# First block of a decoder trunk: squares summed by TensorE, condition vector loaded first, two conditioning rows by TensorE

## The chip, the cores and the metric

One Trainium2 chip, one of its cores. The time is device microseconds of one execution of the whole kernel. The engines named below are TensorE (PE, with its weight loads PEld), VectorE (DVE), ScalarE (ACT), GpSimd (POOL) and SyncE (SP), which issues nearly all transfers. Each engine takes its own instructions in order and waits for the others by semaphores.

## The reference

One layer of a conditioned decoder, 2048 tokens of width 1024. A vector c of width 1024 conditions it: six vectors of 1024 come from one product with a 1024 x 6144 matrix.

```python
c_act = jax.nn.silu(c)
mod = (c_act @ w_ada[l] + b_ada[l])[:, None, :]
sh1, sc1, g1, sh2, sc2, g2 = jnp.split(mod, 6, axis=-1)
h = rms_norm(x) * (1.0 + sc1) + sh1
x = x + g1 * token_mixer(h, w_in[l], ...)
h = rms_norm(x) * (1.0 + sc2) + sh2
x = x + g2 * conv_ffn(h, w_up[l], ...)
return rms_norm(x) * final_gain
```

The change is about the first two lines and the first `rms_norm`, for the first 512 tokens.

## The kernel before

The tokens are taken in four blocks of 512 (`TB`), the width in eight tiles of 128 (`KD`), so x of a block is eight tiles `x[k]` of 128 x 512 with the width on the partitions. Every product with weights is made of three TensorE products of fp32r parts: a weight or activation is split into a high part (a ScalarE cast) and a low part (a VectorE subtraction). `h[k]` holds both parts of the normed, scaled and shifted tile.

The 6144 outputs of the conditioning are 48 columns of 128, called rows here, since row m needs the 128 x 1024 tile `wada[m]` with its outputs on the partitions. `ada(m)` makes one on VectorE: one multiply-and-reduce over 128 x 1024 against `c_act`, which holds the conditioned vector on all partitions, and one short read of the accumulator, into column m of `mod`. Rows 0 to 7 are the shift, 8 to 15 the scale of the first norm; tile k needs rows k and 8 + k.

The first block is done by `startup`, written out by hand in the order in which the code stands; the framework's scheduler then sets each engine's own order by priority, which mostly follows it. In the kernel before it runs so. SP issues the vector of constants `vec`, the table `c_all` (it holds the identity `ident`, a causal mask and `ones`), `craw` (c broadcast to 128 partitions), eight transfers of x, and the first rows and weights, in that order; of SP's transfers eight are under way at a time, and the ninth waits for the first. ScalarE makes the sigmoid of `craw`, VectorE multiplies (`c_act`). ScalarE squares each x tile, VectorE adds it to `acc` (`sumsq`), TensorE sums `acc` over the partitions by four products with `ones`, VectorE makes the reciprocal root by three Newton steps, TensorE spreads it by four transposes, and ScalarE copies it to `bc`. Then for each k: `scaled` (VectorE: x times scale times bc), `high` (ScalarE: add the shift, round), `low` (VectorE: the rest), with conditioning rows and weight splits laid between, and `flush`, which gives TensorE the products that have both operands: with `f` and `q` (512 columns each) and with `v` (256 columns for each of four groups of 128 tokens). Row, weight and tile buffers limit how early loads can start: two raw weight buffers (`NRAW`), three for each part, and eight (`NA4`) for rows, `c_act` and `craw`.

The results stand in four accumulator banks of PSUM. The next product, `pshfh` of unit 1, needs one of them, which ScalarE frees by its two activations `sfh` and `snh` of `pshfh`. From there on the kernel runs in a long fixed sequence of products in which rows 16 to 47 are made between other VectorE work.

Of the kernel before, what the change touches and what calls it, by code (L numbers as in the profile page):

```python
# [10 lines left out]
F32 = mybir.dt.float32  # L11
# [7 lines left out]
P = 128  # L19
D = 1024  # L20
SEQ = 2048
KD = D // P
# [82 lines left out]
def trunk(ctx, tc, xT, vecs, cvec, cst, rope, msk, wada, win, walow, wgla, wout, wup, wdown, out):  # L105
# [37 lines left out]

    vec = pc.tile([P, NV], F32, tag="vec", name="vec")
# [6 lines left out]
    nc.sync.dma_start(c_all[:], cst)  # L151
# [25 lines left out]
    craw = pa.tile([P, D], F32, tag="a4k", name="craw")  # L177
    nc.sync.dma_start(craw[:], cvec.to_broadcast([P, D]))
# [210 lines left out]
    def startup():  # L389


        x, W, pending = [], {}, []
        for k in range(KD):
            x.append(x_tile(f"x0_{k}", k))
            nc.sync.dma_start(x[k], xT[0, :, k, :])
        raws = {}
# [20 lines left out]
        def load(*ms):  # L417
            for m in ms:
                raws[m] = ada_load(m, True)
        load(8, 0)  # L420
        weight("f", 1)
        load(9)
        weight("q", 0)
        load(1, 2)
        acc = new_acc("n1_0")
        for k in range(KD):
            sumsq(acc, x[k], k, "n1_0_")
        cond(8)
        ps = late_ps("ssn1_0")
        for c in range(NCH):  # L430
            T.matmul(ps[:, c:c + 1], acc[:, c * P:(c + 1) * P], ones, start=True, stop=True)
# [3 lines left out]
        cast("f")  # L435
# [4 lines left out]
        cond(0)  # L440
        cond(9)
        S.copy(bc[:], ps[:])
        cast("q")
# [19 lines left out]
        def flush():  # L463
            for q in list(pending):
# [4 lines left out]
        plan = [((10,), (), (1,), "f"), ((3, 11), (), (2,), "q"), ((4,), (10,), (3,), "v0"),  # L469
                ((12, 5), (11,), (4,), None), ((13, 6), (12,), (5,), "v1"), ((14, 7), (13,), (6,), None),  # L470
                ((15,), (14,), (7,), None), ((), (15,), (), None)]
        parts = {"f", "q"}, set()
        for k, (ld, first, then, wl) in enumerate(plan):
            if k == 0:
                weight("v0", 2)
            if k == 3:
                weight("v1", 3, True)
            load(*ld)
            for m in first:
                cond(m)  # L480
            scaled(x[k], bc[:], k)
            high(x[k], k, "0_")
            if k in (1, 4):
                name = "v0" if k == 1 else "v1"
                cast(name)
                parts[0].add(name)
            for m in then:
                cond(m)
            low(x[k], k)
            if wl:  # L490
                low_part(wl)
                parts[1].add(wl)
# [1154 lines left out]
```

## Time and profile before

| | |
|---|---|
| median of 3 runs | 2535.63 us (2533.63 to 2539.6) |
| the profiled execution | 2533.2 us |
| its span | 2531.4 us |
| PE busy | 2452.0 us, 97% |
| PEld busy | 2059.3 us, 81% |
| DVE busy | 1989.5 us, 79% |
| ACT busy | 1147.5 us, 45% |
| POOL busy | 146.3 us, 6% |
| HBM read, written | 397.46 MB, 125.30 MB, 207 GB/s over the span |

The page cuts the span into 40 slices of 63 us. TensorE's busy tenths are 5 in the first slice, 9 in all others but two, which have 8. The chain of work that ended last is TensorE for 82% of the span, VectorE for 8%, transfers for 5%. Matmuls are pipelined, and a row of several lasts from the first's start to the last's end. In a timeline row the bracket tells how long the engine was idle before it and what released it; L numbers are lines of the kernel before.

### The profile page before, as it was taken

How to read it: one execution, taken by the hardware profiler on the slowest of the kernel's cores; microseconds unless marked ns; L12 is line 12 of the kernel's file. 1: busy time of each engine (PE TensorE's matmuls, PEld its weight loads, DVE VectorE, ACT ScalarE, POOL GpSimd, SP SyncE). 2: the span in 40 equal slices, each digit the busy share in tenths (PEclk: the TensorE clock that was granted, in tenths of full speed). 3: DMA queues.
4: the chain of work that ended last, by engine and by line, in shares of the span. 5: the costliest groups of instructions: out<-in, count | busy, mean ns of one | idle time of the engine just before them, and what ended most of it. 6: DMA issues, size and time to landing. Idle time of an engine off the chain costs nothing.

```text
span 2531.4 us, 35178 instructions
## 1 busy us (share of the span) xinstructions
PE 2452.0 (97%) x12165; PEld 2059.3 (81%) x12165; DVE 1989.5 (79%) x3652; ACT 1147.5 (45%) x1950; POOL 146.3 (6%) x278
## 2 busy tenths in 40 slices
PE   5999999999999999999999999999989999999998
PEld 4888877888888888788788888888868888888887
DVE  8987887877688685877798888887678777778666
ACT  3334434434443434434554454455445545545442
POOL 1000000000000000000100000000001010010000
PEclk9999999999999999999999999999999999999999
DMA  8844458865689647884654544587665544447663
GB/s 312 296 159 134 169 169 322 290 234 169 215 283 318 224 157 241 311 300 158 222 190 147 171 147 141 168 283 243 209 199 186 159 137 152 150 133 263 213 196 126
DMA packets 232498, 525.11 MB, mean 207 GB/s; under 512 B 24928, under 2 KB 28032, under 8 KB 232320
## 3 DMA queue, kind: packets, MB, share of 16 engines
q1 hardware_dynamic: 229120, 512.38, 60.0%
q0 software_dynamic: 3200, 10.49, 1.2%
q8 instruction: 96, 1.57, 0.2%
q14 instruction: 82, 0.67, 0.1%
HBM read 397.46 MB, written 125.30 MB: 207 GB/s over the span
## 4 chain that ended last, share of the span: by engine, by line
PE 82%; DVE 8%; DMA 5%; issue 2%; ACT 1%; SPq 0%; DVEq 0%; POOL 0%; ACTq 0%; POOLq 0%
PE X L254 6%; PE X L256 6%; PE X L255 6%; PE Z L256 3%; PE Z L255 3%; PE Z L254 3%; PE lvh L662 3%; PE dX L256 3%; PE dX L255 3%; PE dX L254 3%; PE psqkvgr L254 2%; PE psqkvgr L256 2%; PE psqkvgr L255 2%; PE y L254 2%; PE y L256 2%
## 5 line engine op out<-in xcount | busy, mean ns | idle before, releaser
L254 PE MATMUL X<-B,A 128*128 128x512 f32 x572 | 224.4, 392 | 1.4 <-ACT u L1354 1.4
L255 PE MATMUL X<-B,A 128*128 128x512 f32 x572 | 223.9, 391 | 0.0
L256 PE MATMUL X<-B,A 128*128 128x512 f32 x572 | 223.6, 391 | 0.0
L1055 DVE TENSOR_TENSOR dA<-rd,dA 128x512 fp32r<-128x512 f32 x154 | 106.0, 689 | 87.6 <-ACT dA L1054 87.5
L1054 ACT CAST dA<-rd 128x512 fp32r<-128x512 f32 x154 | 95.6, 621 | 138.8 <-PE dY L256 42.2
L1055 DVE TENSOR_TENSOR A<-s,A 128x512 fp32r<-128x512 f32 x176 | 120.7, 686 | 40.7 <-ACT A L1054 40.3
L1054 ACT CAST A<-s 128x512 fp32r<-128x512 f32 x176 | 108.6, 618 | 68.0 <-PE Z L256 45.2
L254 PE MATMUL dX<-dB,dA 128*128 128x512 f32 x352 | 136.9, 389 | 0.0
L255 PE MATMUL dX<-dB,dA 128*128 128x512 f32 x352 | 136.9, 389 | 0.0
L256 PE MATMUL dX<-dB,dA 128*128 128x512 f32 x352 | 136.9, 389 | 0.0
L254 PEld LDWEIGHTS X<-B,A 128*128 128x128 f32 x572 | 108.2, 189 | 24.5 <-ACT u L1354 2.2
L255 PEld LDWEIGHTS X<-B,A 128*128 128x128 f32 x572 | 108.2, 189 | 22.7
L256 PEld LDWEIGHTS X<-B,A 128*128 128x128 f32 x572 | 108.2, 189 | 22.7
L255 PE MATMUL Z<-B,A 128*128 128x512 f32 x308 | 120.0, 390 | 2.2 <-DVE B L1055 2.2
L254 PE MATMUL Z<-B,A 128*128 128x512 f32 x308 | 119.9, 389 | 0.0
L256 PE MATMUL Z<-B,A 128*128 128x512 f32 x308 | 119.8, 389 | 0.0
L662 PEld LDWEIGHTS lvh<-qbh,kh 128*128 128x128 f32 x768 | 100.5, 192 | 17.0 <-issue 9.2
L1055 DVE TENSOR_TENSOR dB<-rb,dB 128x512 fp32r<-128x512 f32 x154 | 105.6, 686 | 10.2 <-ACT dB L1054 10.1
L1055 DVE TENSOR_TENSOR A<-r,A 128x512 fp32r<-128x512 f32 x130 | 89.3, 687 | 29.4 <-ACT A L1054 29.1
L662 PE MATMUL lvh<-qbh,kh 128*128 128x128 f32 x768 | 102.8, 277 | 7.3 <-DVE kh L672 7.1
L1054 ACT CAST A<-r 128x512 fp32r<-128x512 f32 x130 | 81.0, 623 | 62.4 <-PE Z L256 60.0
L254 PE MATMUL psqkvgr<-hqkvgr,ha 128*128 128x512 f32 x256 | 106.1, 415 | 1.1 <-DVE orsg L160 1.0
(475 smaller groups left out, 6981.2 us busy)
## 6 DMA issues: line engine op xcount, KB each, us to landing
gs<-yv SPq DMA_DIRECT2D x154, 256.0 KB, 2.9
rb<-gs SPq DMA_DIRECT2D x154, 256.0 KB, 3.9
r<-wup SPq DMA_DIRECT2D x140, 256.0 KB, 3.3
s<-sumsu SPq DMA_DIRECT2D x136, 256.0 KB, 3.0
wada<-wada SPq DMA_DIRECT2D x48, 512.0 KB, 6.0
rd<-sumsd SPq DMA_DIRECT2D x88, 256.0 KB, 3.8
rd<-wdown SPq DMA_DIRECT2D x66, 256.0 KB, 3.9
x<-xT SPq DMA_DIRECT2D x64, 256.0 KB, 5.8
```

The costliest lines, as they stand in the source:

```text
L254: T.matmul(ps, lhs[0], rhs[0], start=first, stop=False, skip_group_check=more)
L255: T.matmul(ps, lhs[0], rhs[1], start=False, stop=False, skip_group_check=more)
L256: T.matmul(ps, lhs[1], rhs[0], start=False, stop=last, skip_group_check=more)
L662: T.matmul(ps[:, c * P:(c + 1) * P].rearrange("p (h n s) -> p h n s", h=2, s=s), kq[:, c * P:(c + 1) * P], rhs, start=True, stop=True)
L1054: S.copy(hi, src)
L1055: V.tensor_tensor(lo, src, hi, op=ALU.subtract)
```

## The change

The first transfer is now `craw`, and `c_all` goes out on GpSimd's queue. x comes in four transfers of two tiles each, with the first rows between them. `c_act` is transposed by TensorE into eight columns `ccol`. The squares are no longer added by VectorE: for each tile TensorE multiplies the four 128 x 128 pieces of the square with `ones` and accumulates over the tiles in PSUM. Rows 15 and 7 leave VectorE: `row_spread` transposes the row's tile by TensorE in eight pieces, ScalarE copies them, and `row_sum` multiplies them with the columns of `ccol` in eight products of one column; ScalarE adds the bias. The order inside the tiles is a list of strings (`s` scaled, `c` row, `h` high, `l` low, `l` with a name the low part of that weight).

```diff
+    craw = pa.tile([P, D], F32, tag="a4k", name="craw")
+    nc.sync.dma_start(craw[:], cvec.to_broadcast([P, D]))
     vec = pc.tile([P, NV], F32, tag="vec", name="vec")
     nc.sync.dma_start(vec[:], vecs)
...
-    nc.sync.dma_start(c_all[:], cst)
+    nc.gpsimd.dma_start(c_all[:], cst)
...
-        for k in range(KD):
-            x.append(x_tile(f"x0_{k}", k))
-            nc.sync.dma_start(x[k], xT[0, :, k, :])
+        def x_load(i):
+            x.extend((x_tile(f"x0_{2 * i}", 0), x_tile(f"x0_{2 * i + 1}", 1)))
+            nc.sync.dma_start(pair[0][:].rearrange("p (a n) -> p a n", a=2), xT[0, :, 2 * i:2 * i + 2, :])
...
-        load(8, 0)
+        def row_spread(m):
+            raw, halves = raws.pop(m), []
+            for j in range(2):
+                p = lev_ps(f"wt{m}_{j}")
+                for i in range(4):
+                    T.transpose(p[:, i * P:(i + 1) * P], raw[:, (4 * j + i) * P:(4 * j + i + 1) * P], ident)
+                t = tmp(f"wt{m}_{j}")
+                S.copy(t[:], p[:])
+                halves.append(t)
+            return m, halves
+        def row_sum(m, halves):
+            p = late_ps(f"wm{m}")
+            for i in range(KD):
+                T.matmul(p[:, 0:1], halves[i // 4][:, (i % 4) * P:(i % 4 + 1) * P], ccol[:, i:i + 1],
+                         start=i == 0, stop=i == KD - 1)
+            S.activation(mod[:, m:m + 1], p[:, 0:1], AF.Identity, bias=bada1[:, m:m + 1])
+        load(8)
+        x_load(0)
+        x_load(1)
+        load(0)
+        x_load(2)
+        x_load(3)
+        load(9)
         weight("f", 1)
-        load(9)
+        load(1)
         weight("q", 0)
-        load(1, 2)
-        acc = new_acc("n1_0")
+        load(10, 2)
+        cond(8)
+        for j in range(2):
+            p = lev_ps(f"cc{j}")
+            for i in range(4):
+                T.transpose(p[:, i * P:(i + 1) * P], c_act[:, (4 * j + i) * P:(4 * j + i + 1) * P], ident)
+            S.copy(ccol[:, 4 * j:4 * j + 4], p[:, 0:512:P])
+        ps = late_ps("ssn1_0")
         for k in range(KD):
-            sumsq(acc, x[k], k, "n1_0_")
-        cond(8)
-        ps = late_ps("ssn1_0")
-        for c in range(NCH):
-            T.matmul(ps[:, c:c + 1], acc[:, c * P:(c + 1) * P], ones, start=True, stop=True)
+            sq = late(f"sqn1_0_{k}")
+            S.activation(sq[:], x[k], AF.Square)
+            for c in range(NCH):
+                T.matmul(ps[:, c:c + 1], sq[:, c * P:(c + 1) * P], ones, start=k == 0 and c == 0,
+                         stop=k == KD - 1 and c == NCH - 1, skip_group_check=True)
+        cond(0)
...
-        cond(0)
         cond(9)
+        cast("f")
         S.copy(bc[:], ps[:])
-        cast("q")
...
+        loads = [(11,), (3, 15, 12), (7, 4), (13, 5, 14), (6,), (), (), ()]
+        casts = ["q", "v0", None, "v1", None, None, None, None]
+        steps = ["s0 c1 h lf l c10", "s1 h c2 lq l", "s2 h c11 lv0 l", "s3 c3 h c12 l", "s4 c4 h lv1 l c13",
+                 "s5 c5 h c14 l", "s6 c6 h s7 l", "h l"]
...
             pending += [(kind, k, w) for w in (0, 1) for kind in "fqv"]
+            if rows:
+                row_sum(*rows.pop(0))
+            if k in (3, 4):
+                rows.append(row_spread({3: 15, 4: 7}[k]))
             flush()
```

ScalarE, head of the program, before: the exponential for `lbe`, then the sigmoid of c, then the squares (`san` and `sqn`).

```order
L168 ACT_TABLE_LOAD
L168 ACTIVATE lbe<-lbe 128x4
L179 ACT_TABLE_LOAD
L179 ACTIVATE c_act<-craw 128x1024
L355 ACTIVATE san_0_375<-x_0_345 128x512
L358 ACTIVATE sqn_0_1_377<-x_0_345 128x512
```

ScalarE at the same place in the changed kernel; `cc` is the PSUM tile of the transposed `c_act`.

```order
L180 ACT_TABLE_LOAD
L180 ACTIVATE c_act<-craw 128x1024
L170 ACT_TABLE_LOAD
L170 ACTIVATE lbe<-lbe 128x4
L457 COPY ccol<-cc_375 128x4
L457 COPY ccol<-cc_381 128x4
L461 ACTIVATE sqn_0_0_388<-x_0_348 128x512
L461 ACTIVATE sqn_0_1_394<-x_0_348 128x512
```

The two copies into `ccol` now stand between the sigmoid and the squares, and the two table loads have changed places.

VectorE, the first two tiles, before: `x_0_345` holds tiles 0 and 1, the `wada` rows are conditioning rows 1 and 2, `ha` is the low part of a tile, `lf` and `lq` those of the weights.

```order
L365 SCALAR_TENSOR_TENSOR x_0_345<-x_0_345,mod,bc_0_419 128x512
L199 ISA wada_371,mod<-wada_371,c_act,vec 128x1024
L372 SCALAR_TENSOR_TENSOR ha_0_440<-x_0_345,mod,ha_0_440 128x512
L412 TENSOR_TENSOR lf<-rf,hf 128x1024
L365 SCALAR_TENSOR_TENSOR x_0_345<-x_0_345,mod,bc_0_419 128x512
L199 ISA wada_373,mod<-wada_373,c_act,vec 128x1024
...
L372 SCALAR_TENSOR_TENSOR ha_1_455<-x_0_345,mod,ha_1_455 128x512
```

VectorE at the same place in the changed kernel; `wada_364` is row 1, `wada_370` row 10, `wada_372` row 2.

```order
L366 SCALAR_TENSOR_TENSOR x_0_348<-x_0_348,mod,bc_0_451 128x512
L200 ISA wada_364,mod<-wada_364,c_act,vec 128x1024
...
L413 TENSOR_TENSOR lf<-rf,hf 128x1024
L373 SCALAR_TENSOR_TENSOR ha_0_472<-x_0_348,mod,ha_0_472 128x512
L200 ISA wada_370,mod<-wada_370,c_act,vec 128x1024
...
L366 SCALAR_TENSOR_TENSOR x_0_348<-x_0_348,mod,bc_0_451 128x512
```

`lf` now stands ahead of the low part of tile 0, and row 10 has come ahead of tile 1.

ScalarE, tiles 3 to 5, before: `hv` is the high part of weight v1, `hhfh` that of the next unit's weight.

```order
L369 ACTIVATE ha_3_529<-x_2_348,mod 128x512
L369 ACTIVATE ha_4_557<-x_4_351,mod 128x512
L408 CAST hv_521<-rv_519 128x1024
L242 CAST hhfh_1_722<-rhfh_1_724 128x1024
L369 ACTIVATE ha_5_587<-x_4_351,mod 128x512
```

ScalarE at the same place in the changed kernel; `wt` and `wm` are the PSUM tiles of `row_spread` and `row_sum`, of row 15 first and then of row 7.

```order
L370 ACTIVATE ha_3_567<-x_2_350,mod 128x512
L409 CAST hv_521<-rv_519 128x1024
L430 COPY wt_0_577<-wt_0_572 128x512
L430 COPY wt_1_584<-wt_1_579 128x512
L370 ACTIVATE ha_4_608<-x_4_354,mod 128x512
L439 ACTIVATE mod<-wm_613,vec 128x1
L430 COPY wt_0_628<-wt_0_623 128x512
L430 COPY wt_1_635<-wt_1_630 128x512
L243 CAST hhfh_1_798<-rhfh_1_800 128x1024
L370 ACTIVATE ha_5_657<-x_4_354,mod 128x512
```

The cast of v1 and the copies of row 15 now stand ahead of tile 4, and the sum of row 15, the copies of row 7 and the cast of `hhfh` ahead of tile 5.

## Rows read from the trace of the kernel before

**Rows 1.** Busy time by stretch, us from the span's start; PEclk is the granted clock.

```profile
core 0: us, PE busy (x) PEld busy (x) DVE busy (x) ACT busy (x) POOL busy (x), PEclk, DMA share, GB/s
...
22.50:58.55 36.05, 27.89 (x145) 22.34 (x145) 32.42 (x48) 10.35 (x15) 2.94 (x4) 1.00 0.82 309
58.55:173.40 114.85, 114.21 (x664) 97.99 (x664) 110.05 (x222) 48.59 (x83) 4.05 (x8) 1.00 0.72 251
...
177.10:183.00 5.90, 5.90 (x22) 5.32 (x22) 4.50 (x8) 1.04 (x1) 0.00 (x0) 0.50 0.01 3
```

**Rows 2.** Timeline of the head: start, length, engine, line, instruction, count, idle before.

```profile
1.66 0.42 SPq L178 DMA_DIRECT2D craw<-cvec  x1
...
6.51 1.06 ACT L179 ACTIVATE c_act<-craw 128x1024 f32<-128x1024 f32 x1 [1.92 <-DMA craw<-cvec]
7.60 1.22 DVE L180 TENSOR_TENSOR c_act<-c_act,craw 128x1024 f32<-128x1024 f32 x1 [2.77 <-ACT c_act L179]
...
7.78 0.63 ACT L355 ACTIVATE san<-x 128x512 f32<-128x512 f32 x1 [0.21 <-DMA x<-xT]
...
9.08 5.47 DVE L359 TENSOR_TENSOR san<-san,sqn 128x512 f32<-128x512 f32 x7 [0.25 <-ACT sqn L358]
...
14.60 1.87 PE L431 MATMUL ssn<-c_all,san 128*128 128x1 f32 x8 [14.60 <-DVE san L359]
...
19.84 0.58 ACT L442 COPY bc<-bcn 128x512 f32<-128x512 f32 x1 [2.52 <-PE bcn L439]
...
20.96 0.75 DVE L365 SCALAR_TENSOR_TENSOR x<-x,mod,bc 128x512 f32<-128x512 f32 x1
```

**Rows 3.** Timeline of the first tiles, VectorE and TensorE.

```profile
23.50 1.23 DVE L412 TENSOR_TENSOR lf<-rf,hf 128x1024 fp32r<-128x1024 f32 x1
...
29.57 2.08 PE L459 MATMUL psvgh<-hv,ha 128*128 128x256 f32 x8 [3.86 <-ACT hv L408]
29.73 1.28 DVE L199 CUSTOM_DVE_ANT_0 wada<-wada,c_act,vec 128x1024 f32<-128x1024 f32 x1 [1.13 <-DMA wada<-wada]
...
32.73 0.66 PE L453 MATMUL pshqh<-ha,hq 128*128 128x512 f32 x2
```

**Rows 4.** Timeline of TensorE, the same two products of two tiles running.

```profile
35.92 0.63 PE L453 MATMUL pshfh<-ha,hf 128*128 128x512 f32 x2
...
38.73 0.62 PE L453 MATMUL pshfh<-ha,hf 128*128 128x512 f32 x2
```

**Rows 5.** One-column products: by line (busy, mean ns), and late on the timeline.

```profile
L431 PE MATMUL ssn<-c_all,san 128*128 128x1 f32 x8 | 1.9, 355 | 14.6 <-DVE san L359 14.6
...
2511.89 0.50 PE L1440 MATMUL ssn<-c_all,n3a 128*128 128x1 f32 x4
```

**Rows 6.** Timeline of the first block's end.

```profile
55.23 0.50 PE L453 MATMUL pshfh<-ha,hf 128*128 128x512 f32 x1 [0.55 <-DVE ha L372]
...
57.41 0.60 ACT L742 ACTIVATE sfh<-pshfh 128x512 f32<-128x512 f32 x1 [0.59 <-PE pshfh L453]
...
58.55 0.50 PE L254 MATMUL pshfh<-ha,hhfh 128*128 128x512 f32 x1 [0.48 <-ACT snh L743]
```

**Rows 7.** Timeline around TensorE's longest later wait, VectorE and TensorE.

```profile
143.71 1.23 DVE L247 TENSOR_TENSOR lhqh<-rhqh,hhqh 128x1024 fp32r<-128x1024 f32 x1 [2.80 <-PE uh L701]
...
177.10 0.80 PE L254 MATMUL psvgh<-hvgh,ha 128*128 128x512 f32 x1 [3.66 <-DVE sqh L749]
...
179.82 3.45 PE L662 MATMUL lvg<-qbg,kg 128*128 128x128 f32 x16
```

**Rows 8.** Transfers by line: count, size, median us from issue to landing.

```profile
rhfh<-win SPq DMA_DIRECT2D x1, 512.0 KB, 6.7
...
kepti5l<-lhfh SPq DMA_DIRECT2D x1, 512.0 KB, 3.1
...
hm<-made POOLq DMA_DIRECT2D x16, 256.0 KB, 4.8
```

**Rows 9.** Timeline of ScalarE, a change of table and the activation behind it.

```profile
112.21 1.28 ACT L809 ACT_TABLE_LOAD   x1
113.50 0.73 ACT L809 ACTIVATE ztg<-ztg,c_all 128x512 f32<-128x512 f32 x1
```

More of the change, by code (lines that the diff above doesn't have):

```diff
@@ L176, in trunk @@
     c_act = pa.tile([P, D], F32, tag="a4k", name="c_act")
-    craw = pa.tile([P, D], F32, tag="a4k", name="craw")
-    nc.sync.dma_start(craw[:], cvec.to_broadcast([P, D]))
+    ccol = small("ccol", KD)
     S.activation(c_act[:], craw[:], AF.Sigmoid)
@@ L389, in startup @@
     def startup():
-        x, W, pending = [], {}, []
-        for k in range(KD):
-            x.append(x_tile(f"x0_{k}", k))
-            nc.sync.dma_start(x[k], xT[0, :, k, :])
-        raws = {}
+        x, W, pending, raws = [], {}, [], {}
+        def x_load(i):
+            x.extend((x_tile(f"x0_{2 * i}", 0), x_tile(f"x0_{2 * i + 1}", 1)))
+            nc.sync.dma_start(pair[0][:].rearrange("p (a n) -> p a n", a=2), xT[0, :, 2 * i:2 * i + 2, :])
         def weight(name, i, extra=False):
@@ L434, in startup @@
         newton(ms, r, NCH)
-        cast("f")
         bc = bc1[0] = new_bc1(0)
@@ L467, in flush @@
                     put(*q)
[L469 to L473, printed above, removed]
+        loads = [(11,), (3, 15, 12), (7, 4), (13, 5, 14), (6,), (), (), ()]
+        casts = ["q", "v0", None, "v1", None, None, None, None]
+        steps = ["s0 c1 h lf l c10", "s1 h c2 lq l", "s2 h c11 lv0 l", "s3 c3 h c12 l", "s4 c4 h lv1 l c13",
+                 "s5 c5 h c14 l", "s6 c6 h s7 l", "h l"]
+        parts = {"f"}, set()
+        rows = []
+        for k in range(KD):
             if k == 0:
                 weight("v0", 2)
-            if k == 3:
+            if k == 2:
                 weight("v1", 3, True)
[L478 to L492, printed above, removed]
+            load(*loads[k])
+            for st in steps[k].split():
+                kind, what = st[0], st[1:]
+                if kind == "s":
+                    scaled(x[int(what)], bc[:], int(what))
+                elif kind == "c":
+                    cond(int(what))
+                elif kind == "h":
+                    high(x[k], k, "0_")
+                    if casts[k]:
+                        cast(casts[k])
+                        parts[0].add(casts[k])
+                elif what:
+                    low_part(what)
+                    parts[1].add(what)
+                else:
+                    low(x[k], k)
             pending += [(kind, k, w) for w in (0, 1) for kind in "fqv"]
+            if rows:
+                row_sum(*rows.pop(0))
+            if k in (3, 4):
+                rows.append(row_spread({3: 15, 4: 7}[k]))
             flush()
-        assert not pending
+        assert not pending and not rows
         ready["hfh0_0"], ready["hqh0_0"], ready["vgh0_0"] = pf, pq, pv
```

## The prediction

> **What bounds the kernel now.** I read first the stretches of the whole span [rows 1]. Between 22.5 and 58.55 us TensorE is busy for 27.89 of 36.05 us and VectorE for 32.42; between 58.55 and 173.4 us TensorE is busy for 114.21 of 114.85. So the first block is the only long stretch before the middle in which TensorE waits. Whatever moves the moment at which TensorE begins its unbroken run, 58.55 us, moves the end one for one, unless a later wait absorbs it. I call that moment G. Second, the head in order of time [rows 2]: the condition vector lands, ScalarE and VectorE make c_act, ScalarE squares and VectorE adds, TensorE sums, Newton's steps follow, the rstd is spread to bc, and the first tile is scaled at 20.96. I call that moment T. Third, the first tile [rows 3] and the last [rows 6]: TensorE still waits 0.55 for VectorE's low part in the last tile, so from T to G VectorE is the bound, with 13 conditioning rows, 5 weight splits and 16 passes over x on it. In the kernel before G is T + 37.6; TensorE ends the block 0.48 earlier, at T + 37.1.
>
> **Step 1, c_act.** craw is issued at 1.66 and ScalarE starts on it at 6.51 [rows 2]. In the change it is SP's first issue, and two issues of about 0.46 each no longer stand ahead of it, so it goes out near 0.74. With the same time to landing all of it moves forward by 0.92, and c_act is done at 8.82 - 0.92 = 7.90. The nearest bounds: a 512 KB transfer out of a quiet queue takes 3.1 [rows 8], which would bring c_act 1.75 earlier; and no gain at all, 0.92 later. I take the row of craw itself, since the broadcast stays. c_all, which holds the identity, moves to POOL's queue; transfers there take 4.8 [rows 8], so it lands near 6, some 2 us ahead of c_act, which covers it.
>
> **Step 2, the squares start later.** On ScalarE two copies into ccol now stand before the first square, and they wait for TensorE's eight transposes of c_act. I price these like the eight passes of the old sum, 1.87 [rows 2]: 7.95 to 9.85. A copy of 4 columns I put at 0.3 (512 columns take 0.58 [rows 2]) and a square at 0.63: TensorE starts to sum at 10.8. Before, the first square started at 7.78.
>
> **Step 3, the sum of squares.** Seven additions on VectorE go, 5.47 us for all [rows 2]. TensorE gets 8 x 4 products of a 128x128 block with one column. The row of the old sum shows that four such products are eight passes; they take 1.87 [rows 2], one lasts 0.355 [rows 5], so they start (1.87 - 0.355)/7 = 0.217 apart. The same kind late in the kernel gives 4 passes in 0.50, about 0.11 apart [rows 5]. The first is the lower of the two clock levels, 1.2 GHz, and the second the upper, 2.4 GHz: where the granted clock reads 0.50, sixteen such loads took 3.45, which is 0.21 apart too [rows 1, 7]. So 64 passes cost 64 x 0.217 = 13.9 at the lower level and 7.0 at the upper. ScalarE needs 0.63 a square against 0.88 to 1.74 for its eight passes, so TensorE is the bound of the sum, where VectorE was. The rows ran at the upper level 3.2 us after TensorE started work again at 29.57 [rows 3] and 5.9 us after 177.10 [rows 1, 7]. I take 4.5: 21 passes at the lower level and 43 at the upper, 4.6 + 4.7 = 9.3. The sum ends at 20.1, against 16.47 before.
>
> **Step 4, T.** From the end of the sum to the end of bc's copy took 20.42 - 16.47 = 3.95 [rows 2]. Row 0 is now done on VectorE during the sum, and row 9 while TensorE and ScalarE make bc, so nothing else stands in the way. T = 20.1 + 4.0 = 24.1: 3.1 later.
>
> **Step 5, T to G.** VectorE loses rows 15 and 7, 1.2 each, a wait of 1.13 for a row that came late [rows 3], and the split of the next weight, 1.2: from 34.2 to about 29 us to the last low part. The new bound is TensorE. In its order the products with weight v0 stand right behind tile 0's f and q, in front of tile 1. They need rv, which needs the buffer that lf frees. lf now stands ahead of low 0, a pass of 0.7, so it ends at T + 3.05 instead of T + 3.75; from there to TensorE's start on v took 29.57 - 24.73 = 4.85 [rows 3], so TensorE starts its queue at T + 7.9. The queue: eight tiles of 38.73 - 35.92 = 2.81 [rows 4], less the five 512-column products done before (2560 of a tile's 6144 columns, 1.2), 21.3; sixteen transposes of the two rows at 0.11 [rows 5], 1.8; two sums of sixteen passes, 3.5; and it starts at the lower level as before, 3.2 us at half speed [rows 3], 1.6. Together 28.2, so the block ends at T + 36.1. VectorE's last low part at T + 29 leaves at most two tiles, T + 34.6: TensorE binds. Before, TensorE's queue had seven microseconds of slack, and the extra 5.3 would have been free.
>
> **Step 6, the hand-over.** The sigmoid of c_act now comes before the exponential, so a table load stands on ScalarE in front of the activation that frees the first accumulator. A load takes 1.28 and the next activation follows it at once [rows 9]; 0.59 of idle time stood there [rows 6], so 0.69 is added to the 0.48. By the Trainium skill, page "ScalarE: Activation LUTs", section "What ACT_TABLE_LOAD costs", a switch to another set is about 2.66 us in all, a drain beside the load; the page's table of sets therefore speaks against this order, and by it the sum would be 1.4 higher. The rows at 112.21 and 113.50 show the load alone, so the rows are taken.
>
> G = 24.1 + 36.1 + 1.2 = 61.4, which is **2.8 us later** than 58.55.
>
> **The rest** keeps its order from some 235 VectorE instructions on, and TensorE has no slack to give back, so 2.8 carries to the end. The profiled execution took 2533.2; with the change 2536.0. The median of the runs is 2.4 above that execution: 2538.4.
>
> **Rivals.** (a) The clock stays at the lower level through the whole sum: 13.9 instead of 9.3, place step 3, plus 4.6, in all 7.4 slower: 2543.0. For it: the head shows one-column passes only eight in a row, all at the lower level. Against it: sixteen narrow passes at 179.82 took 3.45, about 0.21 each, and the stretch at the lower level (granted clock 0.50) ended with them [rows 1, 7], so such work did precede a rise. It decides from 43 of the 64 passes at the lower level, since each adds 0.107 to the 7.0 and 2.3 more than forecast makes 0.2%.
> (b) ScalarE in order: hhfh's cast now stands ahead of ha of tile 5. Its data is issued behind row 6, whose buffer TensorE frees only with the transposes of row 15, near T + 17.7. With 6.7 to land [rows 8], cast and ha it is T + 26.6, and TensorE wants ha at about T + 27.4. Slack is 0.8; if the transfer takes some 11 us, as behind a full queue, it costs 4: 2542.4.
> (c) The sum runs at the upper rate from its first pass: 7.0, so plus 0.5 in all: 2536.1. Only [rows 5] speaks for it; the head's row is at the lower rate.
> By the Trainium skill, page "TensorE: Matmul & The Clock Gate", section "LDWEIGHTS (loading the stationary operand)", a load of 128 columns takes 107 ns whatever the clock. By that, an estimate of 64 x 0.107 = 6.8 for the sum, the result would be (c). The trace agrees with it at 2512 us only; at 14.60 the same passes are twice as far apart.
> (d) VectorE's relief reaches the wait at 173.4 to 177.1, which costs 3.66 and then 5.9 us at half speed, about 6.6 [rows 1, 7]: 2.8 - 6.6 = 3.8 faster, 2531.8. Against it: at 143.71 VectorE itself waits 2.80 for TensorE [rows 7], which erases any lead, and its order is unchanged after that.
>
> **How the numbers follow.** Chances: forecast 0.50, (a) 0.25, (b) 0.08, (c) 0.07, (d) 0.10. 0.2% is 5.1 us, about what a measurement of this kernel can tell from no change. Slower by that: 0.20 of (a), 0.06 of (b), and 0.06 of the forecast, with a late craw and a late rise together. Faster by that: a third of (d), and 0.03 of the forecast and (c) for runs that scatter. The forecast's own bounds are -1.75 (craw), -0.7 and +0.7 (the rise), +0.9 (craw unmoved), and -1.6 if TensorE enters the loop at the upper level; with the scatter of the runs that is 2533 to 2541.5. To take in most of (a) and (b) and half of (d), the range is 2532 to 2544.5.
>
> **What would show it.** Step 1: c_act's activation starts near 5.6. Step 2: the first square starts near 10.2. Step 3: the eight-pass groups are 1.7 apart at first and 0.9 later, and the last ends near 20; if they stay 1.7 apart, it is (a). Step 4: first scaling near 24. Step 5: from the start on v0 TensorE has no idle time until the block's end, and its next product starts near 61; idle time on VectorE's low parts would refute it, idle time on ha of tile 5 would be (b). Step 6: an idle TensorE of about 1.2 there. Wrong altogether if G is before 57.

## The result: slower by 0.21%, and the profile after

The median is 2540.96 us (2537.61 to 2543.96), beside 2534.94 (2532.66 to 2539.6) for the kernel before on the same chip. The ratio is 1.0021, interval 1.0014 to 1.0027, which is 5.3 us, 3.5 to 6.8; the medians are 6.0 apart. The forecast was 2538.4, 2.8 slower; the measured time lies between it and rival (a), 7.4 slower. The profiled execution took 2540.03 with a span of 2538.0, against 2533.2 and 2531.4.

The head of the changed kernel in the timeline (start, length, engine, line, instruction, count, idle before and what ended it). It answers to [rows 2].

```profile
4.78 1.06 ACT L180 ACTIVATE c_act<-craw 128x1024 f32<-128x1024 f32 x1 [2.76 <-DMA craw<-cvec]
...
7.15 1.97 PE L456 MATMUL cc<-c_all,c_act 128*128 128x128 f32 x8 [7.15 <-DVE c_act L181]
...
9.68 1.15 ACT L461 ACTIVATE sqn<-x 128x512 f32<-128x512 f32 x2 [0.36 <-DMA x<-xT]
...
10.36 13.81 PE L463 MATMUL ssn<-c_all,sqn 128*128 128x1 f32 x64 [1.24 <-ACT sqn L461]
...
12.32 0.63 ACT L461 ACTIVATE sqn<-x 128x512 f32<-128x512 f32 x1 [1.49 <-PE ssn L463]
...
20.86 0.63 ACT L461 ACTIVATE sqn<-x 128x512 f32<-128x512 f32 x1 [1.09 <-PE ssn L463]
...
28.17 0.75 DVE L366 SCALAR_TENSOR_TENSOR x<-x,mod,bc 128x512 f32<-128x512 f32 x1 [0.62 <-ACT bc L475]
```

The one row that carries the result is the sum: 64 passes in 13.81, which is (13.81 - 0.355)/63 = 0.214 apart from the first to the last. The squares show the same from the other side. ScalarE has two buffers for them, so from the third on it waits for TensorE, and they follow each other 1.7 apart to the end. T, the first scaling, is 28.17 instead of 20.96.

From T on, the same kernel's timeline of TensorE and of the engines that it depends on, in answer to [rows 3], [rows 4] and [rows 6].

```profile
35.88 2.07 PE L491 MATMUL psvgh<-hv,ha 128*128 128x256 f32 x8 [1.82 <-ACT hv L409]
...
49.39 1.84 PE L437 MATMUL wm<-ccol,wt 128*128 128x1 f32 x16
51.10 1.07 PE L428 MATMUL wt<-c_all,wada 128*128 128x128 f32 x8
...
54.44 0.75 DVE L373 SCALAR_TENSOR_TENSOR ha<-x,mod,ha 128x512 fp32r<-128x512 f32 x1 [1.21 <-ACT ha L370]
...
63.93 1.28 ACT L782 ACT_TABLE_LOAD   x1
...
64.54 0.62 PE L491 MATMUL psvgh<-lv,ha 128*128 128x256 f32 x4
...
64.56 1.23 DVE L248 TENSOR_TENSOR lhqh<-rhqh,hhqh 128x1024 fp32r<-128x1024 f32 x1 [4.10 <-PE pshfh L485]
...
65.23 0.60 ACT L782 ACTIVATE sfh<-pshfh 128x512 f32<-128x512 f32 x1
...
66.36 0.50 PE L255 MATMUL pshfh<-ha,hhfh 128*128 128x512 f32 x1 [1.20 <-ACT snh L783]
```

TensorE works from 35.88 to 65.16 with no idle row between, VectorE waits 4.10 for it at the end, and a table load stands in front of `sfh`. G, TensorE's first product of the next unit, is 66.36 instead of 58.55, 7.8 later. The span is 6.6 longer. So 7.2 of the 7.8 arose ahead of T, and in these two executions about 1.2 were given back behind G.

To follow what becomes of G, one more point is used below: M, the product behind TensorE's longest later wait, which stands at 177.10 in [rows 7], G + 118.6. In the changed kernel:

```profile
153.23 1.23 DVE L248 TENSOR_TENSOR lhqh<-rhqh,hhqh 128x1024 fp32r<-128x1024 f32 x1 [3.95 <-PE uh L741]
...
186.61 0.50 PE L255 MATMUL psvgh<-hvgh,ha 128*128 128x512 f32 x1 [3.66 <-DVE sqh L789]
```

M is G + 120.3. In both kernels M comes 33.4 behind the end of VectorE's wait for `uh`, a product of TensorE.

### The profile page after: what moved, and what is told of

Same layout as the page of the kernel before. It is cut to its first block, busy times and chain, and to the rows that moved or that the text cites. A ratio compares the mean times of both kernels' runs of the same rounds, so it can differ in the third digit from the quotient of the medians.

```text
span 2538.0 us, 35408 instructions
## 1 busy us (share of the span) xinstructions
PE 2468.9 (97%) x12277; PEld 2078.4 (82%) x12277; DVE 1982.4 (78%) x3641; ACT 1150.6 (45%) x1959; POOL 147.1 (6%) x279
## 4 chain that ended last, share of the span: by engine, by line
PE 83%; DVE 7%; DMA 6%; issue 2%; ACT 1%; SPq 0%; DVEq 0%; POOL 0%; ACTq 0%; POOLq 0%
PE X L255 6%; PE X L257 6%; PE X L256 6%; PE Z L256 3%; PE Z L257 3%; PE Z L255 3%; PE lvh L702 3%; PE dX L257 3%; PE dX L256 3%; PE dX L255 3%; PE psqkvgr L255 2%; PE psqkvgr L257 2%; PE psqkvgr L256 2%; PE y L255 2%; PE y L257 2%
## 5 line engine op out<-in xcount | busy, mean ns | idle before, releaser
L255 PE MATMUL Z<-B,A 128*128 128x512 f32 x308 | 119.9, 389 | 0.0
L1095 DVE TENSOR_TENSOR dB<-rb,dB 128x512 fp32r<-128x512 f32 x154 | 105.3, 685 | 10.2 <-ACT dB L1094 10.2
```

The costliest lines, as they stand in the source:

```text
L255: T.matmul(ps, lhs[0], rhs[0], start=first, stop=False, skip_group_check=more)
L1095: V.tensor_tensor(lo, src, hi, op=ALU.subtract)
```

## The experiments

All but two start from the changed kernel. A ratio is given where a kernel was timed several times beside the kernel before; the other four rest on the trace of one execution each.

### VectorE sums the squares again

```diff
+        acc = new_acc("n1_0")
+        for k in range(KD):
+            sumsq(acc, x[k], k, "n1_0_")
         ps = late_ps("ssn1_0")
-        for k in range(KD):
-            sq = late(f"sqn1_0_{k}")
-            S.activation(sq[:], x[k], AF.Square)
-            for c in range(NCH):
-                T.matmul(ps[:, c:c + 1], sq[:, c * P:(c + 1) * P], ones, ...)
+        for c in range(NCH):
+            T.matmul(ps[:, c:c + 1], acc[:, c * P:(c + 1) * P], ones, start=True, stop=True)
```

> The changed kernel with one part undone: VectorE adds the squares again and TensorE sums only the total, four products of one column. Theory, the sum's 64 one-column passes at the lower clock level are what moved T from 20.96 to 28.17: VectorE starts to add when it has done row 8 and the four short steps behind it, near 11.0, the seven additions take 5.5, the four products 1.9, and the chain to bc 3.9, so T is near 22.3, TensorE's unbroken run starts 7.7 later near 30.0, G is near 60.5, and the time is about 6 us below the changed kernel's 2540.0, near 2534. Rival, T is late because of the other edits of the head (the order of the transfers, the copies into ccol): T stays above 26, and the time stays above 2538.

The timeline of this kernel:

```profile
17.15 1.87 PE L463 MATMUL ssn<-c_all,san 128*128 128x1 f32 x8 [7.63 <-DVE san L360]
...
23.01 0.75 DVE L366 SCALAR_TENSOR_TENSOR x<-x,mod,bc 128x512 f32<-128x512 f32 x1 [0.62 <-ACT bc L474]
...
60.53 0.50 PE L255 MATMUL pshfh<-ha,hhfh 128*128 128x512 f32 x1 [1.20 <-ACT snh L782]
```

T falls from 28.17 to 23.01 (22.3 expected) and G from 66.36 to 60.53 (60.5). The ratio to the kernel before is 1.0005 (0.9992 to 1.0018). The sum on TensorE is 5.2 of the 7.2 by which T was late. The other edits of the head leave T 2 us later than in the kernel before: VectorE's additions start at 10.79 instead of 9.08, after 0.82 of waiting for squares that stand behind the copies into `ccol` on ScalarE, and end at 17.1 instead of 14.5, with another wait of 0.94 for the square of a tile that lands later.

### Wide products ahead of the sum

```diff
+        d = acc_ps("wide")
+        for i in range(6):
+            T.matmul(d[:], ident, c_act[:, 0:512], start=i == 0, stop=i == 5)
         ps = late_ps("ssn1_0")
```

> The changed kernel with six products of 512 columns (the identity with c_act, fp32, result not used) on TensorE between the transposes of c_act and the sum. Extra work that only shows the clock. They take 1.7 each at the lower level and 0.85 at the upper, so they start near 9.1 and the sum starts between 15 and 19.5. Theory 1, one-column products don't raise the level by themselves, but they run at the upper level where the work ahead of them has raised it: the eight groups of the sum are then 0.9 apart, 7 to 8 us for the sum, T near 27 to 29. Theory 2, in the head TensorE stays at the lower level whatever it does, and the level comes later for another reason: the wide products stay 1.7 apart, the groups stay 1.7 apart, the sum takes 13.8 and T is 34 to 37. Theory 3, the level rises with the wide products and falls back under the narrow ones: the first groups 0.9 apart, the later ones 1.7, T between the two.

Two views of this kernel, first the timeline of TensorE and ScalarE:

```profile
9.14 7.23 PE L460 MATMUL wide<-c_act,c_all 128*128 128x512 f32 x12
16.20 10.50 PE L466 MATMUL ssn<-c_all,sqn 128*128 128x1 f32 x64
...
18.14 0.63 ACT L464 ACTIVATE sqn<-x 128x512 f32<-128x512 f32 x1 [0.27 <-PE ssn L466]
19.06 0.63 ACT L464 ACTIVATE sqn<-x 128x512 f32<-128x512 f32 x1 [0.29 <-PE ssn L466]
...
21.67 0.63 ACT L464 ACTIVATE sqn<-x 128x512 f32<-128x512 f32 x1 [1.07 <-PE ssn L466]
23.39 0.63 ACT L464 ACTIVATE sqn<-x 128x512 f32<-128x512 f32 x1 [1.09 <-PE ssn L466]
```

and the busy time by stretch, with the columns of [rows 1]; the first number in brackets counts TensorE's passes, and the granted clock stands third from the end:

```profile
17.50:19.00 1.50, 1.50 (x15) 1.50 (x15) 0.00 (x0) 1.00 (x2) 0.00 (x0) 1.00 1.03 410
...
21.00:22.00 1.00, 1.00 (x6) 1.00 (x6) 0.00 (x0) 0.33 (x1) 0.00 (x0) 0.50 0.17 62
```

It is theory 3. The wide products brought the level up, so the head as such does not keep it down. The sum began at the upper level, ten passes to the microsecond, and squares 0.9 apart. Near 20 us, with nothing but one-column passes since 16.20, the granted clock fell to 0.50: six passes to the microsecond, and squares 1.7 apart. T is 30.70, between the two other theories. So one-column passes neither raised the level in the 13.8 us of the changed kernel nor kept it here once it was up. The forecast's step 3 had needed both.

### Sixty-four columns instead of one

```diff
-                T.matmul(ps[:, c:c + 1], sq[:, c * P:(c + 1) * P], ones, ...)
+                T.matmul(ps[:, c * 64:(c + 1) * 64], sq[:, c * P:(c + 1) * P], ones.to_broadcast([P, 64]), ...)
...
```

> The changed kernel with the same 64 passes of the sum, each with 64 columns of ones instead of one (63 of them are not used). Loads and passes are as many as before; only more columns move. Theory, the level follows how much moves through the array, not how long TensorE is busy: the groups begin 1.7 apart and go on 0.9 apart, the sum takes 9 to 10 and T is near 24. Rival, 64 columns are still too few, or the level follows something else: all groups 1.7 apart or more, the sum takes 13.8 or longer and T is at 28 or later.

```profile
10.23 13.91 PE L463 MATMUL ssn<-c_all,sqn 128*128 128x64 f32 x64 [0.78 <-ACT sqn L461]
```

The rival holds: 64 columns cost no more than one (13.91 against 13.81), and the level stayed low all the same. T is 28.14.

### The sum turned round

```diff
...
+            T.matmul(pw1[0:1, :], ones, sq[:], start=k == 0, stop=k == KD - 1)
+        row = tmp("rown1_0", (1, 512))
+        S.copy(row[:], pw1[0:1, :])
...
+        for c in range(NCH):
+            T.matmul(ps[:, c:c + 1], row[:, c * P:(c + 1) * P], ones[0:1, :], start=True, stop=True)
```

> The changed kernel with the sum of squares turned round: the column of ones is the loaded operand and the squares move, 512 columns to a product, eight products of two passes; the row of sums is copied by ScalarE and turned into four columns by four one-column products. At the lower level 16 passes of 0.86 are 13.7, as long as the one-column form; at the upper 0.43 each. Theory, wide work raises the level and one-column work doesn't: the first four or five passes at 0.86, the rest at 0.43, the sum of about 9 ends near 19.5 instead of 24.2, and with 2.5 for the copy and the four products T is near 26. Rival, the level in the head doesn't follow the kind of work: all passes 0.86, the sum ends near 24 and T is near 30.5.

```profile
10.86 8.76 PE L462 MATMUL wsn<-sqn,c_all 128*1 128x512 f32 x16 [1.50 <-ACT sqn L461]
...
14.45 0.63 ACT L461 ACTIVATE sqn<-x 128x512 f32<-128x512 f32 x1 [1.05 <-PE wsn L462]
15.31 0.63 ACT L461 ACTIVATE sqn<-x 128x512 f32<-128x512 f32 x1 [0.23 <-PE wsn L462]
...
24.87 0.75 DVE L366 SCALAR_TENSOR_TENSOR x<-x,mod,bc 128x512 f32<-128x512 f32 x1 [0.16 <-ACT bc L478]
...
62.97 0.50 PE L255 MATMUL pshfh<-ha,hhfh 128*128 128x512 f32 x1 [1.20 <-ACT snh L786]
```

As expected: squares 1.7 apart up to 14.45 and 0.86 from there, 8.76 for the sum; T came 1.1 earlier than the 26 expected. At the lower level both forms of the sum would take about the same, an estimate of 13.7 from sixteen times 0.86 against 13.8 measured; only the wide one got out of it. T is 3.3 earlier than in the changed kernel and G 3.4. It still loses to VectorE's sum by 1.9 at T.

### Rows 15 and 7 back on VectorE

```diff
-        loads = [(11,), (3, 15, 12), (7, 4), (13, 5, 14), (6,), (), (), ()]
+        loads = [(11,), (3, 12), (4,), (13, 5), (14, 15), (6, 7), (), ()]
...
-                 "s5 c5 h c14 l", "s6 c6 h s7 l", "h l"]
+                 "s5 c5 h c14 l c15", "s6 c6 h s7 c7 l", "h l"]
...
-            if rows:
-                row_sum(*rows.pop(0))
-            if k in (3, 4):
-                rows.append(row_spread({3: 15, 4: 7}[k]))
```

> The changed kernel with rows 15 and 7 back on VectorE, and their loads in the order of use; the head stays. Theory, TensorE is the bound from T to G, and the rows' transposes and sums (5.8 us in the trace of the changed kernel) are on its path: T stays near 28.2; VectorE then has 13 rows, 16 passes over x and 4 weight splits, about 31 us, and a last tile's products of some 2.5 behind them, so G moves from T + 38.2 to about T + 35, that is from 66.4 to about 63.4, with idle time of TensorE on VectorE's low parts back in the last tiles, and the time falls by about 3, to 2537. Rival, something else holds the loop at T + 38 (the weights' transfers, the first accumulator): G stays at 66 and the time at 2540.

The timeline of this kernel at the block's end:

```profile
57.48 0.50 PE L485 MATMUL pshfh<-ha,hf 128*128 128x512 f32 x1 [0.99 <-ACT ha L370]
...
58.45 1.63 DVE L373 SCALAR_TENSOR_TENSOR ha<-x,mod,ha 128x512 fp32r<-128x512 f32 x2
...
59.26 0.65 PE L485 MATMUL pshfh<-ha,hf 128*128 128x512 f32 x1 [1.28 <-DVE ha L373]
...
60.56 1.91 PE L491 MATMUL psvgh<-hv,ha 128*128 128x256 f32 x8
...
67.64 0.50 PE L255 MATMUL pshfh<-ha,hhfh 128*128 128x512 f32 x1 [1.20 <-ACT snh L779]
```

and the busy time by stretch there (PEclk stands third from the end):

```profile
58.90:61.00 2.10, 1.74 (x6) 1.45 (x7) 1.97 (x3) 0.40 (x1) 0.00 (x0) 0.63 0.35 144
61.00:63.00 2.00, 2.00 (x9) 1.87 (x9) 0.22 (x1) 0.00 (x0) 0.00 (x0) 0.53 0.49 193
```

The expectation failed: T is 28.83 and G T + 38.8, no earlier than in the changed kernel (T + 38.2), and the ratio is 1.0025 (1.0013 to 1.0038). The bound did move: TensorE now waits for VectorE and ScalarE. But VectorE made the low parts of the last two tiles together, after the last rows, so two tiles of products were still to come, and behind the two waits the granted clock was 0.63 and 0.53, with TensorE's rows up to twice as long (eight products with `v` in 1.91, where 1.12 is usual in the block). That stretch took 7.2, 59.26 to 66.4, where I had put 2.5. So TensorE's extra work in the loop is not a pure addition: it filled time that an order of this kind leaves idle. What it costs against a better order is seen further down.

### The vector of constants first

```diff
+    vec = pc.tile([P, NV], F32, tag="vec", name="vec")
+    nc.sync.dma_start(vec[:], vecs)
     craw = pa.tile([P, D], F32, tag="a4k", name="craw")
     nc.sync.dma_start(craw[:], cvec.to_broadcast([P, D]))
-    vec = pc.tile([P, NV], F32, tag="vec", name="vec")
-    nc.sync.dma_start(vec[:], vecs)
```

> The changed kernel with the first two transfers exchanged: the vector of constants first, the condition vector second, so that the exponential runs ahead of the sigmoid as in the kernel before. Theory, the table load of 1.28 in front of the activation that frees the first accumulator is what made TensorE's idle time at G 1.20 instead of 0.48: no table load stands there, the idle time is 0.48 again, c_act starts about 0.46 later, and G is near 66.1. Rival, the idle time has another cause (the order of ScalarE's casts there): it stays at 1.2 and G is near 66.8.

```profile
64.95 0.60 ACT L782 ACTIVATE sfh<-pshfh 128x512 f32<-128x512 f32 x1 [0.59 <-PE pshfh L485]
...
66.09 0.50 PE L255 MATMUL pshfh<-ha,hhfh 128*128 128x512 f32 x1 [0.48 <-ACT snh L783]
```

No table load stands in front of `sfh`, and the idle time at the hand-over is 0.48 again, as in [rows 6]. G is 66.09, as expected. The table load costs 0.72 there. The Trainium skill, page "ScalarE: Activation LUTs", section "What ACT_TABLE_LOAD costs", puts a switch at about 2.66 with its drain; by that, an estimate of 2.66 less the 0.59 of idle time, 2.1 would have been added, and the measurement decides for the load alone.

### The kernel before, with a delay

This is the only way to ask what a later G costs with nothing else changed.

```diff
+        for i in range(11):
+            V.tensor_tensor(acc[:], acc[:], acc[:], op=ALU.max)
+        V.scalar_tensor_tensor(ms[:], acc[:, 0:NCH], 0.0, ms[:], op0=ALU.mult, op1=ALU.add)
         newton(ms, r, NCH)
```

> The kernel before with a pure delay: eleven passes of VectorE over the sum of squares (128 x 512 each, they change nothing) between the sum and Newton's steps, some 7.6 us. All that follows keeps its order. It asks how much of a delay of G is left at the end. Theory, a delay of G carries to the end one for one: G moves from 58.55 to about 66.2 and the time by 7.6, to about 2541. Rival, the long sequence behind G takes some of a delay back, as the changed kernel seems to show (G 7.8 later, the span 6.6 longer, the medians 5.4 apart): the time moves by 5 to 6.5, to about 2538.5 to 2540.

```profile
66.44 0.50 PE L254 MATMUL pshfh<-ha,hhfh 128*128 128x512 f32 x1 [0.48 <-ACT snh L746]
...
185.13 0.50 PE L254 MATMUL psvgh<-hvgh,ha 128*128 128x512 f32 x1 [3.66 <-DVE sqh L752]
```

G is 7.9 later, M comes at G + 118.7 as in the kernel before, so up to M a delay is carried one for one. The ratio is 1.0024 (1.0013 to 1.0036), 6.1 us, 3.3 to 9.1. The interval holds both theories, and the changed kernel's 5.3 at a G of 7.8 later is in it. So the comparison gives no sign that the changed kernel's other edits gave anything back by themselves; whether the long sequence behind M returns one or two microseconds of any delay can't be told at this precision. How far single executions scatter shows here: in the profiled execution of this kernel the span is 9.6 longer than in the kernel before, with G only 7.9 later.

### A version put together from these

VectorE sums, x goes out right behind `vec` and `craw`, all rows are on VectorE, and the low parts of the last tiles are not pushed behind later rows.

```diff
-        load(8)
         x_load(0)
         x_load(1)
-        load(0)
         x_load(2)
         x_load(3)
-        load(9)
+        load(8, 0, 9)
...
-                 "s5 c5 h c14 l", "s6 c6 h s7 l", "h l"]
+                 "s5 c5 h c14 l c6", "s6 h c7 l c15", "s7 h l"]
```

> A version put together from the experiments: VectorE adds the squares, x goes out right behind the vector of constants and the condition vector, the table of constants stays on GpSimd's queue, all rows are on VectorE, the low part of f stands ahead of tile 0's, and the low parts of tiles 5 to 7 are not pushed behind rows of later tiles. Theory: squares start near 6.8, the sum ends near 15.5, T is near 19.5 to 20; VectorE binds from T to G with 31 to 32 and one tile behind it, T + 34.7, the hand-over waits 0.5, so G is near 55 against 58.55, and the time falls by 2 to 3.5 us if G carries to the end. Rival, the rows' transfers are the bound of the first block (the DMA engines are full there): VectorE waits for rows, G stays at 57 or later and the time within 1.5 us of the kernel before.

The timeline of this kernel:

```profile
21.40 0.75 DVE L365 SCALAR_TENSOR_TENSOR x<-x,mod,bc 128x512 f32<-128x512 f32 x1 [0.62 <-ACT bc L466]
...
57.30 0.50 PE L254 MATMUL pshfh<-ha,hhfh 128*128 128x512 f32 x1 [0.48 <-ACT snh L770]
...
142.07 0.77 PE L254 MATMUL pshfh<-ha,hhfh 128*128 128x512 f32 x1 [3.17 <-DVE sgg L588]
...
184.15 0.80 PE L254 MATMUL psvgh<-hvgh,ha 128*128 128x512 f32 x1 [3.67 <-DVE sqh L776]
```

From T to G it takes 35.9 against 37.6 in the kernel before and 38.2 in the changed one, so this order of the loop is the better one. x in transfers of two tiles came in later, the first square starts at 8.47 instead of 7.78, and T is 21.40, where 19.5 to 20 were expected. G is 1.25 earlier than before, not 3.5. The rival's 57 fits, but not its cause: from T to G VectorE waits only for ScalarE's `ha`, 0.32 and 0.79, and never for a row. And yet M is 7 us later, and the ratio is 1.0016 (1.0002 to 1.0031). The expected gain is a loss. Between G and M TensorE waited 7.1 for VectorE in five waits (1.22, 0.58, 1.36, 0.74 and the 3.17 above), where the kernel before has 0.6.

### Where the combined version loses

In its trace VectorE waited in turn for casts of weights that came late, 0.80, 0.91 and 1.43 (3.1 together; the first expectation below has 7.6 in five waits, which the trace does not show), and on SP the write of a low part, which waits for VectorE, stood ahead of a load. Two ways to take the write out of the load's way were tried. The first sends all writes of low parts out on GpSimd's queue; beside the combined version the kernel before and the changed kernel got the same edit, for comparison.

```diff
-        nc.sync.dma_start(kept[key][:], t.bitcast(F32))
+        nc.gpsimd.dma_start(kept[key][:], t.bitcast(F32))
```

The combined version, with x in eight transfers:

> The combined version again, with two edits: the low parts that are written back to memory go out on GpSimd's queue, so that on SP they no longer stand ahead of the next weights' loads, and x comes in eight transfers. In the combined version TensorE reached G at 57.30, 1.25 earlier than in the kernel before, but the product behind TensorE's wait of 3.7 for the next unit's q (177.10 in the kernel before) came at 184.15, G + 126.9 instead of G + 118.6; VectorE waited 7.6 in five waits between for casts of weights that had come late, and on SP the write of a low part, which waits for VectorE, stood ahead of the load. Theory, that order is what the gain was lost to: T is near 20.8, G near 56.7, the product comes at G + 118 to 120, 175 to 177, and the time is 1 to 2.5 below the kernel before. Rival, VectorE simply has too much work behind G, whatever the loads do: the product comes at 181 or later and the time is not below that of the kernel before.

The kernel before:

> The kernel before with one edit: the low parts are written back on GpSimd's queue instead of SP's. It is the comparison for the run beside it. Theory, in the kernel before the write stood behind the next load, so nothing waited for it: G stays at 58.5, the product behind the wait of 3.7 at 177, the time within 1.5 of the kernel before. Rival, the write in front of later loads or GpSimd's own queue matters: the product moves by more than 2, either way, and the time with it.

The changed kernel:

> The changed kernel with the same one edit. In the changed kernel the write of a low part stands ahead of the load of the next weight on SP, TensorE waits 2.3 in three waits for VectorE between G and the product behind the wait of 3.7, and that product comes at G + 120.3 instead of G + 118.6. Theory, the order of SP's transfers costs these 1.7: the product comes at G + 118.5, near 184.9, and the time falls by about 1.7 from 2540. Rival, the waits come from VectorE's own order: the product stays at G + 120 or later, and the time at 2540 or above.

The edit itself is bad, and all three theories failed: the ratios are 1.0065 (1.0051 to 1.0079), 1.0081 (1.0068 to 1.0093) and 1.0096 (1.0082 to 1.0109), and G is 61.64, 63.73 and 71.06, 4 to 5 us later than in the same kernels without the edit. In the kernel before there are four waits of TensorE in the last tiles, and between M and the end another 17 us go, some 14 of them between 432 and 520 us; their cause is not shown. As a comparison among the three it still says something. M comes at G + 119.7, 120.5 and 119.9: the combined version no longer loses between G and M. VectorE's order has changed with the edit too, though, in a place that is taken up below. Among themselves the medians are 2550.51, 2554.66 and 2559.59, so with this edit the changed kernel is again the slowest, by 4.9, and the combined version, with x in eight transfers, the fastest by 4.2.

The second way keeps SP and gives each write out one weight later:

```diff
             nc.sync.dma_start(raw[:], src)
+            while owed:
+                keep(*owed.pop())
...
-                keep(key + "l", lo[:])
+                owed.append((key + "l", lo[:]))
```

> The combined version once more, x in eight transfers, all transfers on SP again. One edit: the write of a low part is given out one weight later, behind the load of the next weight, so that SP has the load of unit 1's last v weight ahead of the write of the low part that was ahead of it in the combined version. The runs with the writes on GpSimd's queue had G to the product behind TensorE's wait of 3.7 at 120 in all three kernels, but G itself 3 to 5 later. Theory, the load behind the write was what the combined version lost behind G: T is near 20.8, G near 56.7, the product comes at G + 118.5 to 120, near 176, and the time is 1 to 3 below the kernel before. Rival, VectorE has too much to do behind an early G, whatever stands in SP's order: the product comes at 181 or later and the time is not below that of the kernel before.

The timeline:

```profile
57.90 0.50 PE L258 MATMUL pshfh<-ha,hhfh 128*128 128x512 f32 x1 [0.48 <-ACT snh L775]
...
139.24 0.47 PE L258 MATMUL pshfh<-ha,hhfh 128*128 128x512 f32 x1 [3.17 <-DVE sgg L593]
...
181.35 0.79 PE L258 MATMUL psvgh<-hvgh,ha 128*128 128x512 f32 x1 [3.66 <-DVE sqh L781]
```

T is 21.34 and G 57.90, for 20.8 and 56.7 expected. The loss between G and M falls from 8.3 to 4.9. The three waits of the combined version between 86 and 103 us, 3.2 together, are down to one of 0.20, and VectorE waits for no cast any more, so the place of the writes was part of it, as far as x in eight transfers, the other difference, was not.

The rest is mostly the wait of 3.17 for `sgg`, which the combined version has too. `sgg` is a product of a gate and its sigmoid on VectorE; eight of them free the accumulators. The number of the rival came true, M at 181 or later, but the cause is not how much VectorE has to do. From 57.4 to the last `sgg` it runs the same 164 instructions in both kernels, busy for 81.87 in the kernel before and 81.72 here, and it is done at 140.9 before and at 139.7 here. What differs is the order. In the kernel before two `sgg` are made at 134.82 and three more ahead of a conditioning row:

```profile
135.95 0.68 DVE L561 TENSOR_TENSOR sgg<-sgg,psvgg 128x128 f32<-128x128 f32 x3
136.55 1.28 DVE L199 CUSTOM_DVE_ANT_0 wada<-wada,c_act,vec 128x1024 f32<-128x1024 f32 x1
```

and TensorE starts the product that waits here at 136.59, with no idle time. In this kernel three are made at 134.74, and the other five stand behind the row, two steps on `qbh` and `kh` and the low part of a weight:

```profile
135.33 1.27 DVE L199 CUSTOM_DVE_ANT_0 wada<-wada,c_act,vec 128x1024 f32<-128x1024 f32 x1
...
138.61 1.08 DVE L593 TENSOR_TENSOR sgg<-sgg,psvgg 128x128 f32<-128x128 f32 x5
```

So TensorE's product starts 2.65 later than before, though VectorE is done with the whole 1.2 earlier. Behind the wait the granted clock was 0.50 from 140.15 to 143.57, and 1.6 more are lost up to M. In the combined version with its writes on GpSimd's queue five `sgg` are made ahead of such work (136.91 to 138.7), and TensorE has no such wait. The 0.7 by which G is earlier is lost there; a version with the order of before at this place was not tried. The ratio is 1.0021 (1.0011 to 1.0031). None of the versions beat the kernel before.

## Why the prediction was right or wrong, point by point

The time was inside the range and the direction of the likeliest case right, but its size came out 2.5 too small, and at G the error was 5: the likeliest case was not the one that happened. That the time fell inside the range shows little, since the range was drawn to take in most of (a). The error at G, 66.36 for 61.4, is made up of -0.4 at the start of the sum, +4.5 in the sum, nothing up to T, +0.9 from T to the end of the block and nothing at the hand-over. That about half of it is seen in the time is luck: the prediction let G carry to the end unchanged.

**Step 1** held. c_act started at 4.78, 0.8 earlier than priced, and `c_all` on GpSimd's queue was there when TensorE wanted it. **Step 2** held in its number: first square at 9.68 for 10.2, sum from 10.36 for 10.8. But the copies into `ccol` were done early, by 9.3, and what the first square waited for last was the transfer of x, 0.36, which the step had left out.

**Step 3** failed, and it is the mis-sized term: 13.81 for 9.3. The choice of 4.5 us to a rise was taken from rows of wide products (29.57 in [rows 3], 177.10 in [rows 7]) and laid on one-column products. The evidence against it was in view: the only one-column rows of the head were at the lower level. The row that tipped the choice, sixteen narrow passes at 179.82 that ended with a rise, had six wide products in front of it. The kernel with wide products ahead of the sum shows what such a sequence did here: the level rose under the wide products and fell under the narrow ones. This is rival (a) with its place and its price, the whole sum at the lower level, 13.9; by it G would have been 66.0. Its 7.4 in the time did not come, since less than G's delay was left at the end. By the Trainium skill, page "TensorE: Matmul & The Clock Gate", section "LDWEIGHTS (loading the stationary operand)", a load takes its columns divided by 1.2 in ns, 107 for 128 columns, with no term for the clock; an estimate from that, 6.8, gave rival (c). The rows at 10.36 to 24.17, 0.214 apart, speak against it.

**Step 4** held exactly: 4.0 from the end of the sum to T.

**Step 5** held in its mechanism. TensorE started on v0 at T + 7.7 (7.9), had no idle row from there on, and ended at T + 37.0 (36.1). Most of the 0.9 is the start: the products stayed at the lower level to about 41 us, 5.5 us where 3.2 were priced. The rows' transposes and sums took 2.1 and 3.7 (1.8 and 3.5). Rival (b) appeared, since VectorE waited 1.21 for `ha` of tile 5 behind the cast of `hhfh`, and was hidden under TensorE as its slack had it. That TensorE was the bound in this order is thus shown. That the two rows on it were a loss of their full 5.8 is not: the kernel without them gained nothing, and an order that suits VectorE gained 2.3 of T to G, 0.7 of it from the hand-over.

**Step 6** held: 1.20 at the hand-over, and 0.48 without the table load.

**The rest** was wrong in a small way. G was carried on to M with 1.7 added, as TensorE waited 2.3 for VectorE (0.6 in the kernel before), and some 3 us were returned behind M, so that 7.8 at G became 6.6 in the spans and 5.3 in the ratio. 1.1 of it is seen at once: from M to TensorE's next wait of more than a microsecond (1.89, which ends at 308.96 before and at 317.38 after) it takes 131.9 before and 130.8 after. In the first stretch behind M the granted clock was 0.50 over 5.90 us [rows 1], and in the changed kernel 0.66 over 5.06:

```profile
186.61:191.67 5.06, 5.06 (x23) 4.80 (x24) 4.50 (x8) 1.05 (x1) 0.00 (x0) 0.66 0.05 19
```

Further on TensorE of the kernel before waits four times for VectorE's `kh`, 0.54, 0.46 and 0.81 at 422 to 433 us and 1.25 at 1002, and the changed kernel's trace has none of these waits. The remainder is within what single executions scatter, and whether other executions return as much stays open. **Rival (d)** is refuted: the wait of 3.66 is unchanged, and VectorE's own wait ahead of it grew from 2.80 [rows 7] to 3.95.

## What to carry to other kernels

Before moving a reduction to TensorE, count its passes at the clock level that such passes have at that place, not at the level of the wide products nearby: here 64 one-column passes in a row ran at the lower level to the last, and where wide products had raised the level they did not hold it. Where the sum must be on TensorE, let the data move and keep the ones still: that took 8.76 instead of 13.81 here, though VectorE's sum was still better by 1.9 at T. And follow a gain to the next hand-over between two engines, and read the order there: behind G VectorE was busy for nearly all of 83 us in every order, and five short products behind a row and a weight split, instead of ahead of them, took back more than the 0.7 that G had gained.

## What was not expected of the hardware

- 64 passes of one column, 13.8 us of TensorE without a pause, stayed at the lower level throughout; the same number with 64 columns stayed there too, in 13.91. In the sum of eight wide products of two passes the level rose part of the way through, between the squares at 14.45 and 15.31.
- The granted clock reads 1.00 over a whole stretch in which the passes are 0.214 apart. A stretch of the changed kernel's sum, with 20 passes in 4 us:

```profile
14.00:18.00 4.00, 4.00 (x20) 4.00 (x21) 0.00 (x0) 1.81 (x3) 0.00 (x0) 1.00 1.03 413
```

  In these traces the column shows a fall, as at 21 us in the kernel with wide products ahead, but not that the level has yet to rise for the first time; for that only the distance of the passes served.
- Moving the writes of the low parts, 512 KB each in the first block, from SP's queue to GpSimd's made the kernel before some 20 us slower (ratio 1.0081). Why is not shown.
